# Equal SBUF offsets for all pools, and token sums made amid the first steps of the second pair

## The chip, the cores and the metric

The kernel runs on one core of one Trainium2 chip. The metric is the device time of an execution in microseconds (us); the times of several runs are given by their median. Instructions run on five engines with a queue each: TensorE (PE, with its weight loads shown apart as PEld), VectorE (DVE), ScalarE (ACT), GpSimd (POOL) and SyncE (SP), which issues the DMAs here. L211 means line 211 of the kernel.

## What is computed

One decoder layer over x of 1024 tokens by 1024 features, all in float32: a SwiGLU feed-forward with half weight, a token mixer (four heads of a gated delta rule and four of gated linear attention), a second SwiGLU, and a normalisation after each.

```python
def _swiglu(x, w_gate, w_up, w_down):
    return (jax.nn.silu(x @ w_gate) * (x @ w_up)) @ w_down
...
        x = _layer_norm(ALPHA * x + 0.5 * _swiglu(x, ffn1_w_gate[i], ffn1_w_up[i], ffn1_w_down[i]),
                        ln1_g[i], ln1_b[i])
        mix = _token_mixer(x, w_in[i], conv_w[i], a_log[i], dt_bias[i], gdn_norm_w[i],
                           w_gk[i], b_gk[i], gla_norm_w[i], w_out[i])
        x = _layer_norm(ALPHA * x + mix, ln2_g[i], ln2_b[i])
        x = _layer_norm(ALPHA * x + 0.5 * _swiglu(x, ffn2_w_gate[i], ffn2_w_up[i], ffn2_w_down[i]),
                        ln3_g[i], ln3_b[i])
```

The feed-forward width is 2816, which is 22 blocks of 128.

## The kernel before

**Products.** Every float32 operand is split into a high part, rounded to TensorE's fp32r (L131, on ScalarE), and the rest, the low part (L132, on VectorE). A product is three matmuls: high by high, high by low, low by high. Nearly all have 128 rows, 128 stationary columns and 512 moving columns. In a matmul the stationary tile is loaded first (PEld), then the moving tile streams past it. `proj` (L189, L190, L192) holds weights `wh`, `wl` and streams x (`xh`, `xl`). `down` (L211 to L213) holds a hidden tile (`gh`, `gl`; `hh`, `hl` in the middle; for one of the last blocks `fh`, `fl` stand in the place of the weights' halves) and streams the down weights `wh`, `wl`; its result is added to `acc` by VectorE (L216).

**Stages.** Blocks 0 and 1 of the first feed-forward are made plainly (block 0 by `hidden_first`, block 1 by `hidden`); then ten blocks go in pairs (`ffn_pairs`); then ten single blocks, whose second half fills the gaps of the token mixer (the middle of the program); then the second feed-forward: single blocks for one half of the tokens, five pairs, and four last blocks.

**Pairs.** Two blocks by two halves of the tokens are a 2x2 block product of gates and one of ups, made with seven projections in place of eight (Winograd's form; `PRODUCTS` lists P1 to P7). Four of the seven stream sums of x over the tokens: P3, P5 and P6 from `token_sums(q)` for q = 0 to 3, which loads four pieces of x and makes three sums, and P7 from `last_sums`, which overwrites the x tiles `xh10` to `xh13`, `xl10` to `xl13` with the differences. Each sum is split by `sum_parts`. The weights of a pair are sums too (`weight_sums`). `TURNS` sets the order of the steps of a pair by hand: g is one projection of the gates, u one of the ups, d one down step of the pair before.

```python
TURNS = "ggddddgddddgddddgddddgguuuuuuu"
```

Weights are made up to `DEEP` = 4 steps ahead of the step that asks for them.

**Order.** Each engine runs its queue in order. The framework's scheduler makes the queues: it starts from the order in which the calls in `run` issue the instructions and lets some pass others whose operands come later by its own model; the loads of `acc` are exempt (`keep_in_program_order`). Loads into scratch tiles `wr` (seven buffers) wait until a buffer is free.

**Memory.** `wt` takes a tile from a pool. Tiles are laid one behind the other in units of 32 bytes. The pools that stay open are `cp` (with `mhalf`), `xp` (`acc`, x and P7), `wp` (weights and `wr`) and `sl` (small statistics); behind them the phases open and close theirs: `fs` (token sums), `fa` and `fb` (hidden tiles of the pairs), `hp`, `mp` and others (the middle). By the addresses of the built program, the tiles of `xp` and `wp` begin 32 past a multiple of 64, those of `fs`, `fa`, `fb` and `hp` at a multiple of 64.

Of the kernel before, what the change touches and what calls it, by code (L numbers as in the profile page):

```python
# [39 lines left out]
C_END = C_SEL + 2  # L40
# [4 lines left out]
K1, K2 = 12, 8  # L45
# [5 lines left out]
LAST = 4  # L51
# [35 lines left out]
class Layer:  # L87
# [22 lines left out]
    def bank(self, tag):  # L110
        return self.ps.tile([P, HT], F32, name=self.nm(tag), tag=tag, bufs=BANKS[tag])

    def wt(self, pool, shape, tag, bufs, dt=F32):
        return pool.tile([P] + shape, dt, name=self.nm(tag), tag=tag, bufs=bufs)

    def u(self, tag, pool=None):
        return self.wt(pool or self.mp, [HT], tag, BUFS[tag])
# [26 lines left out]

    def constants(self, cp):
        nc = self.nc
        self.cst = cp.tile([P, C_END], F32, name="cst")
        self.ident = self.cst[:, C_ID:C_ID + P]
        self.lncol = cp.tile([P, 48], F32, name="lncol")
        self.msk = cp.tile([P, MASKW], U8, name="msk")  # L150
        self.small = cp.tile([P, 52], F32, name="small")
        self.rowb = cp.tile([P, 8], F32, name="rowb")
        self.wgk = cp.tile([P, 2 * P], F32, name="wgk")

    def load_constants(self):
        nc, a = self.nc, self.a
        nc.sync.dma_start(self.cst[:], a["cst"])
        nc.sync.dma_start(self.lncol[:], a["lncol"])
        for j in range(0, MASKW, HT):
            w = min(HT, MASKW - j)  # L160
            raw = self.u("wr", self.wp)
            nc.sync.dma_start(raw[:, 0:w], a["msk"][:, j:j + w])
            nc.scalar.copy(self.msk[:, j:j + w], raw[:, 0:w])
        nc.sync.dma_start(self.small[:], a["small"])
        nc.sync.dma_start(self.rowb[:], a["row"].partition_broadcast(P))
        nc.sync.dma_start(self.wgk[:], a["wgk"])
        nc.vector.tensor_scalar(self.small[:, 0:50], self.small[:, 0:50], 0.5, None, ALU.mult)
        nc.scalar.activation(self.rowb[:, 4:8], self.rowb[:, 4:8], AF.Exp)
# [6 lines left out]
        self.nc.sync.dma_start(raw, self.a["xT"][half, k])  # L175
        self.split(h[:], l[:], raw)

    def load_acc(self, c):
        self.tc.keep_in_program_order(self.nc.sync.dma_start(self.acc[c][:], self.a["x"][c]))

    def proj(self, w, half):
        nc = self.nc
# [237 lines left out]

    def sum_parts(self, n, q, t):

        pool, tags = (self.xp, (f"xh1{q}", f"xl1{q}")) if n == "P7" else (self.fs, (f"{n}{q}h", f"{n}{q}l"))
        self.sx[n, q] = [self.wt(pool, [HT], t, 1, F32R) for t in tags]
        self.split(self.sx[n, q][0][:], self.sx[n, q][1][:], t[:])

    def load(self, src):
# [11 lines left out]
        for n, t in (("P6", s2), ("P5", s1), ("P3", s4)):  # L439
            self.sum_parts(n, q, t)  # L440

    def last_sums(self):

        for q in range(KB // 2):
            s3, a21 = [self.load(self.raw_x(i, q)) for i in range(2)]
            self.nc.vector.tensor_tensor(s3[:], s3[:], a21[:], ALU.subtract)
            self.sum_parts("P7", q, s3)

    def tokens(self, n):
        x = lambda half, j: [(self.xh[half][k], self.xl[half][k]) for k in range(4 * j, 4 * j + 4)]  # L450
# [107 lines left out]
                self.split(hl[0][:], hl[1][:], raw[:])  # L558
                yield hl

    def ffn_pairs(self, idx, fs, before=None):

        gu, wd = self.a[f"gu{idx}"], self.a[f"wd{idx}"]
        order = [n for n, b in PRODUCTS]
        turns, need = [], []

        def plan(f, before, kinds):

            hid, work, asks = {}, {}, {}
            if before:  # L570
                keys = [(n, d) for d in range(2) for n in range(2)]
                asks["d"] = [keys[:2]] + [[]] * 7 + [keys[2:]] + [[]] * 7
                work["d"] = {}, before[1], self.halves_of([wd[before[0] + n] for n in range(2)])
            if f is not None:
                for up in range(2):

                    blocks = [m[:, sl] for sl in HALVES for m in (gu[f, up], gu[f + 1, up])]
                    asks["gu"[up]] = [[n] for n in order]
                    work["gu"[up]] = {}, hid, self.weight_sums(order[4:], *blocks)
            makes = {k: self.down_turns(w[0], w[1]) if k == "d" else self.project(w[0], w[1], k == "u") for k, w in work.items()}  # L580
            for make in makes.values():
                next(make)
            for kind in kinds:
                if kind in work:
                    ops, _, weights = work[kind]
                    for n in asks[kind].pop(0):
                        need.append((ops, n, weights))
                    turns.append((makes[kind], len(need)))
            return f, hid

        for f in range(fs.start, fs.stop, 2):
            before = plan(f, before, TURNS)
        plan(None, before, "d" * 16)
        made = 0
        for make, asked in turns:
            while made < min(asked + DEEP, len(need)):
                ops, n, weights = need[made]
                ops[n] = next(weights)
                made += 1
            next(make, None)  # L600

    def chunk(self, t, c):
# [447 lines left out]
        return on, half, 4 + 2 * p, 21 + 6 * p, self.small[:, 49:50]  # L1050

    def run(self):
        self.mhalf = self.cp.tile([P, 4], F32, name="mhalf")
        self.nc.gpsimd.memset(self.mhalf[:], -0.5)
        self.halo, self.S, self.SB = {}, [None] * NH, [None] * 2
        for c in range(KB):
            self.acc[c] = self.wt(self.xp, [D], f"acc{c}", 1)
        with self.phase("fs") as self.fs, self.phase("fa") as self.fx:
            self.scr = "gs", self.fx
            hs = [self.hidden_first(self.fx, ("gh", "gl"), 4)]  # L1060
            for q in range(KB // 2):
                self.token_sums(q)
            hs.append(now(self.hidden(1, 1, (0, 1), self.fx, ("gh", "gl"), 4)))
            for c in range(KB):
                self.load_acc(c)
            self.last_sums()
            self.ffn_pairs(1, range(2, K1), (0, {f"{i + 1}{j + 1}": hs[j][i] for i in range(2) for j in range(2)}))
        with self.phase("hp") as self.hp, self.phase("kp") as kp, self.phase("sp") as self.sp, self.phase("mp") as self.mp:
            self.scr = "xf", self.hp
            self.constants(kp)  # L1070
            self.load_constants()
            for k in range(KB // 2):
                self.restore(1, k)
            self.middle()
        with self.phase("fs") as self.fs, self.phase("fb") as self.fx:
            self.scr = "gs", self.fx
            for q in range(KB // 2):
                now(self.ffn(2, range(q * K2 // 4, (q + 1) * K2 // 4), 1, True))
                self.token_sums(q)
            self.last_sums()  # L1080
            self.ffn_pairs(2, range(K2, NF - LAST))
        self.last_blocks(range(NF - LAST, NF))

    def middle(self):
# [112 lines left out]
```

## Time and profile before

| | |
|---|---|
| time, median of 3 runs | 2081.43 us (2080.74 to 2082.23) |
| the profiled execution's own time | 2077.97 us |
| its span | 2075.8 us |
| TensorE busy | 2039.1 us in 10052 instructions |
| VectorE busy | 1443.4 us in 3057 |
| ScalarE busy | 785.9 us in 1553 |
| TensorE's granted clock, mean | 0.997 of full speed |
| read from HBM | 171.74 MB, 87 GB/s with what is written |

The profile is one execution. "Busy" of TensorE counts the time in which any matmul is in flight; matmuls overlap, so how quickly they follow one another is read from the starts in the timeline and not from the durations. A share of the chain is the part of the span in which that engine was what the end waited for.

### The profile page before, as it was taken

The page shows a single profiled execution, that of the slowest core. Times are in us where ns is not written, and L with a number is a line of the kernel's source. Part 1 is how long each engine was busy: PE and PEld are TensorE (multiplying, and loading weights), DVE is VectorE, ACT ScalarE, POOL GpSimd, SP SyncE. Part 2 cuts the span into 40 slices and gives each one's busy share as a digit, 9 for nine tenths or more (in the row PEclk, how much of TensorE's full clock was granted, in tenths as well). Part 3 has the DMA queues.
Part 4 walks back from the last instruction along what each step waited for, and adds up shares of the span by engine and source line. Part 5 has one row for each costly group of instructions (what it writes and reads, how often), then busy time and mean ns, then how long its engine had stood idle before and what let it go on. Part 6 is the DMA issues. An engine that isn't in the chain of part 4 may idle for free.

```text
span 2075.8 us, 27622 instructions
## 1 busy us (share of the span) xinstructions
PE 2039.1 (98%) x10052; PEld 1651.6 (80%) x10052; DVE 1443.4 (70%) x3057; ACT 785.9 (38%) x1553; POOL 54.8 (3%) x87
## 2 busy tenths in 40 slices
PE   7999999999999999999999999999999999999998
PEld 6888888888888777788788777788788788888887
DVE  6665565555688888768899888778856656556566
ACT  5333333223354444434464444343433322333332
POOL 0000000000000000000101000000000000000000
PEclk9999999999999999999999999999999999999999
DMA  8311112332322212222242222122444311112331
GB/s 305 106 46 61 52 51 62 121 94 91 101 92 81 69 60 84 64 67 91 68 147 67 72 72 72 61 72 75 139 132 132 97 56 46 62 51 87 120 114 66
DMA packets 97481, 181.94 MB, mean 88 GB/s; under 512 B 11200, under 2 KB 11712, under 8 KB 97344
## 3 DMA queue, kind: packets, MB, share of 16 engines
q1 hardware_dynamic: 97344, 180.17, 27.3%
q8 instruction: 79, 1.29, 0.3%
q14 instruction: 58, 0.48, 0.1%
HBM read 171.74 MB, written 8.39 MB: 87 GB/s over the span
## 4 chain that ended last, share of the span: by engine, by line
PE 87%; DVE 7%; ACT 2%; issue 2%; DMA 1%; POOL 1%; SPq 0%; DVEq 0%; ACTq 0%; POOLq 0%
PE pa L189 11%; PE pa L190 11%; PE pa L192 11%; PE pd L212 9%; PE pd L211 9%; PE pd L213 9%; PE pm L528 3%; PE pm L529 3%; PE pm L530 3%; PE pa L529 3%; PE pa L528 3%; PE pa L530 3%; PE pm L1019 1%; PE pm L617 1%; DVE wl L132 1%
## 5 line engine op out<-in xcount | busy, mean ns | idle before, releaser
L131 ACT CAST wh<-wr 128x512 fp32r<-128x512 f32 (+1 forms) x593 | 366.8, 620 | 891.0 <-PE pa L190 289.1
L132 DVE TENSOR_TENSOR wl<-wr,wh 128x512 fp32r<-128x512 f32 (+1 forms) x593 | 405.1, 686 | 240.7 <-ACT wh L131 238.3
L189 PE MATMUL pa<-xh,wh 128*128 128x512 f32 x1168 | 469.5, 402 | 15.0 <-ACT wh L131 6.0
L190 PE MATMUL pa<-xl,wh 128*128 128x512 f32 x1168 | 462.1, 396 | 0.1
L192 PE MATMUL pa<-xh,wl 128*128 128x512 f32 x1152 | 456.2, 396 | 0.0
L216 DVE SCALAR_TENSOR_TENSOR acc<-pd,acc 128x512 f32<-128x512 f32 x433 | 293.5, 686 | 97.4 <-PE pd L213 93.2
L189 PEld LDWEIGHTS pa<-xh,wh 128*128 128x128 f32 x1168 | 221.2, 189 | 62.8 <-ACT wh L131 6.7
L190 PEld LDWEIGHTS pa<-xl,wh 128*128 128x128 f32 x1168 | 221.1, 189 | 43.7 <-DVE xl L132 1.8
L192 PEld LDWEIGHTS pa<-xh,wl 128*128 128x128 f32 x1152 | 217.2, 189 | 43.8 <-DVE wl L132 0.5
L211 PE MATMUL pd<-wh,gh 128*128 128x512 f32 (+1 forms) x450 | 176.9, 394 | 1.2 <-ACT gh L131 1.0
L212 PE MATMUL pd<-wl,gh 128*128 128x512 f32 (+1 forms) x450 | 178.1, 396 | 0.0
L213 PE MATMUL pd<-wh,gl 128*128 128x512 f32 (+1 forms) x450 | 176.6, 393 | 0.0
L211 PE MATMUL pd<-wh,hh 128*128 128x512 f32 x352 | 142.0, 408 | 1.7 <-ACT xf L260 1.5
L212 PE MATMUL pd<-wl,hh 128*128 128x512 f32 x352 | 141.1, 401 | 1.0 <-DVE wl L132 1.0
L213 PE MATMUL pd<-wh,hl 128*128 128x512 f32 x352 | 138.4, 399 | 0.0
L211 PEld LDWEIGHTS pd<-wh,gh 128*128 128x128 f32 x450 | 84.5, 188 | 23.4 <-ACT gh L131 2.2
L213 PEld LDWEIGHTS pd<-wh,gl 128*128 128x128 f32 x450 | 84.5, 188 | 20.8 <-DVE gl L132 0.6
L212 PEld LDWEIGHTS pd<-wl,gh 128*128 128x128 f32 x450 | 84.5, 188 | 19.6
L211 PEld LDWEIGHTS pd<-wh,hh 128*128 128x128 f32 x352 | 66.3, 189 | 20.3 <-ACT hh L131 3.7
L213 PEld LDWEIGHTS pd<-wh,hl 128*128 128x128 f32 x352 | 66.0, 188 | 15.8 <-DVE hl L132 2.1
L212 PEld LDWEIGHTS pd<-wl,hh 128*128 128x128 f32 x352 | 66.5, 189 | 14.5 <-DVE wl L132 1.9
L528 PE MATMUL pm<-xh,wh 128*128 128x512 f32 x160 | 63.3, 396 | 0.0
(452 smaller groups left out, 3060.8 us busy)
## 6 DMA issues: line engine op xcount, KB each, us to landing
wr<-gu SPq DMA_DIRECT2D x263, 256.0 KB, 2.6
wr<-wd SPq DMA_DIRECT2D x132, 256.0 KB, 2.6
wr<-win SPq DMA_DIRECT2D x116, 256.0 KB, 2.6
wr<-wout SPq DMA_DIRECT2D x32, 256.0 KB, 2.6
wr<-xT SPq DMA_DIRECT2D x28, 256.0 KB, 4.9
wr<-x2d SPq DMA_DIRECT2D x28, 256.0 KB, 2.7
acc<-xT SPq DMA_DIRECT2D x16, 256.0 KB, 5.4
acc<-x SPq DMA_DIRECT2D x8, 512.0 KB, 9.3
```

The costliest lines, as they stand in the source:

```text
L131: self.nc.scalar.copy(hi, src)
L132: self.nc.vector.tensor_tensor(lo, src, hi.bitcast(F32), ALU.subtract)
L189: nc.tensor.matmul(ps[:], hi[:, sl], xh[k][:], start=(k == 0), stop=False)
L190: nc.tensor.matmul(ps[:], hi[:, sl], xl[k][:], start=False, stop=(lo is None and k == KB - 1))
L192: nc.tensor.matmul(ps[:], lo[:, sl], xh[k][:], start=False, stop=(k == KB - 1))
L211: nc.tensor.matmul(p, hh[:, sl], wh[:, ds], start=(i == 0), stop=False)
L212: nc.tensor.matmul(p, hh[:, sl], wl[:, ds], start=False, stop=False)
L213: nc.tensor.matmul(p, hl[:, sl], wh[:, ds], start=False, stop=(i == n - 1))
L216: nc.vector.scalar_tensor_tensor(acc, p, scale / ALPHA, acc, ALU.mult, ALU.add, accum_out=None if sums is None else sums[:, d:d + 1])
L528: nc.tensor.matmul(ps[:], op[0][:, sl], xh[:], start=new, stop=False, skip_group_check=True)
L529: nc.tensor.matmul(ps[:], op[0][:, sl], xl[:], start=False, stop=False, skip_group_check=True)
L530: nc.tensor.matmul(ps[:], op[1][:, sl], xh[:], start=False, stop=q == 3, skip_group_check=True)
```

## The change

Two things are changed.

First the layout. `wt` pads every tile to 16 elements (64 bytes for float32) unless it is told another unit; `mhalf` and the constants are widened likewise. By the addresses of the built program all tiles then begin at multiples of 64, those of x and weights at multiples of 128, hidden tiles 64 past one. An exception is written out: the sums P3, P5 and P6 are taken with 8 elements (32 bytes) more and the unit 8, so that high parts begin at a multiple of 64 and the low parts that follow 32 past one.

Then the order. In the first feed-forward `token_sums`, the loads of `acc` (now two halves of 256 KB each per tile) and `last_sums` are handed to `ffn_pairs` as `beside`: turn t of the steps first runs what `beside` has for t. In turns 0 to 3 these are the sums of q = t and the first halves of two `acc` tiles, in turns 6 to 9 the second halves of two and the differences of P7. So block 1's weights are loaded directly behind x. In the second feed-forward `last_sums` goes beside turns 0 to 3, behind the first weights of the pair.

```diff
-    def wt(self, pool, shape, tag, bufs, dt=F32):
-        return pool.tile([P] + shape, dt, name=self.nm(tag), tag=tag, bufs=bufs)
+    def wt(self, pool, shape, tag, bufs, dt=F32, line=16):
+
+        n = int(np.prod(shape))
+        if n % line == 0:
+            return pool.tile([P] + shape, dt, name=self.nm(tag), tag=tag, bufs=bufs)
+        t = pool.tile([P, n + -n % line], dt, name=self.nm(tag), tag=tag, bufs=bufs)[:, 0:n]
+        return t if len(shape) == 1 else t.rearrange("p (a b) -> p a b", b=shape[1])
...
-    def load_acc(self, c):
-        self.tc.keep_in_program_order(self.nc.sync.dma_start(self.acc[c][:], self.a["x"][c]))
+    def load_acc(self, c, d):
+        ds = HALVES[d]
+        self.tc.keep_in_program_order(self.nc.sync.dma_start(self.acc[c][:, ds], self.a["x"][c][:, ds]))
...
-        pool, tags = (self.xp, (f"xh1{q}", f"xl1{q}")) if n == "P7" else (self.fs, (f"{n}{q}h", f"{n}{q}l"))
-        self.sx[n, q] = [self.wt(pool, [HT], t, 1, F32R) for t in tags]
+        if n == "P7":
+            self.sx[n, q] = [self.wt(self.xp, [HT], f"x{e}1{q}", 1, F32R) for e in "hl"]
+        else:
+            self.sx[n, q] = [self.wt(self.fs, [HT + 8], f"{n}{q}{e}", 1, F32R, 8)[:, 0:HT] for e in "hl"]
...
-        for make, asked in turns:
+        for t, (make, asked) in enumerate(turns):
             while made < min(asked + DEEP, len(need)):
                 ops, n, weights = need[made]
                 ops[n] = next(weights)
                 made += 1
+            for work in beside.get(t, ()):
+                work()
             next(make, None)
...
-        self.mhalf = self.cp.tile([P, 4], F32, name="mhalf")
+        self.mhalf = self.cp.tile([P, 32], F32, name="mhalf")
...
-            for q in range(KB // 2):
-                self.token_sums(q)
             hs.append(now(self.hidden(1, 1, (0, 1), self.fx, ("gh", "gl"), 4)))
-            for c in range(KB):
-                self.load_acc(c)
-            self.last_sums()
-            self.ffn_pairs(1, range(2, K1), (0, {f"{i + 1}{j + 1}": hs[j][i] for i in range(2) for j in range(2)}))
+            hid = {f"{i + 1}{j + 1}": hs[j][i] for i in range(2) for j in range(2)}
+            beside = {t: [lambda q=t: self.token_sums(q)] for t in range(KB // 2)}
+            for t in range(4):
+                beside[t] += [lambda c=c: self.load_acc(c, 0) for c in (2 * t, 2 * t + 1)]
+                beside[6 + t] = [lambda c=c: self.load_acc(c, 1) for c in (2 * t, 2 * t + 1)]
+                beside[6 + t].append(lambda q=t: self.last_sums(q))
+            self.ffn_pairs(1, range(2, K1), (0, hid), beside)
...
-            self.last_sums()
-            self.ffn_pairs(2, range(K2, NF - LAST))
+            self.ffn_pairs(2, range(K2, NF - LAST), beside={t: [lambda q=t: self.last_sums(q)] for t in range(KB // 2)})
```

`last_sums` takes q now and does one of its four rounds per call. Lines move by five to seven: L131 and L132 become L136 and L137, L211 to L213 become L217 to L219, L328 becomes L334, L436 to L438 become L444 to L446, L446 becomes L453, L528 to L530 become L535 to L537.

How the instructions move is shown at three places. The first is VectorE at the start: before, directly behind block 0's low parts, the token sums are made (L436 to L438, and the low parts P50l, P60l, P30l), ahead of anything of block 1.

```order
L132 TENSOR_TENSOR xl_55_192<-acc_8_81,xh_54_191 128x512
L132 TENSOR_TENSOR gl_250<-gs_221,gh_249 128x512
L436 TENSOR_TENSOR wr_310<-wr_310,wr_312 128x512
L437 TENSOR_TENSOR wr_314<-wr_310,wr_314 128x512
L132 TENSOR_TENSOR P50l_326<-wr_310,P50h_325 128x512
L438 TENSOR_TENSOR wr_316<-wr_316,wr_314 128x512
L132 TENSOR_TENSOR P60l_322<-wr_314,P60h_321 128x512
L436 TENSOR_TENSOR wr_333<-wr_333,wr_335 128x512
L132 TENSOR_TENSOR P30l_330<-wr_316,P30h_329 128x512
L437 TENSOR_TENSOR wr_337<-wr_333,wr_337 128x512
```

Now they come behind block 1's up weights, amid its gate products (L334) and the weights of the pair.

```order
L137 TENSOR_TENSOR wl_473<-wr_470,wh_472 128x512
L444 TENSOR_TENSOR wr_483<-wr_483,wr_485 128x512
L137 TENSOR_TENSOR P50l_499<-wr_483,P50h_498 128x512
L334 TENSOR_TENSOR gs_347<-gs_347,pa_388 128x512
L445 TENSOR_TENSOR wr_487<-wr_483,wr_487 128x512
L137 TENSOR_TENSOR gl_415<-gs_347,gh_414 128x512
L137 TENSOR_TENSOR P60l_495<-wr_487,P60h_494 128x512
L137 TENSOR_TENSOR wl_480<-wr_476,wh_479 128x512
L446 TENSOR_TENSOR wr_489<-wr_489,wr_487 128x512
L334 TENSOR_TENSOR gs_374<-gs_374,pa_418 128x512
L137 TENSOR_TENSOR wl_525<-wr_448,wh_524 128x512
L137 TENSOR_TENSOR P30l_503<-wr_489,P30h_502 128x512
```

All of q = 0 has moved behind some forty instructions of block 0 and 1, and the others follow in the next turns. The second place is TensorE at the end of the first P6 of the pairs; P62 and P63 are its third and fourth sum. Before, the step runs through and a down step follows.

```order
L528 MATMUL pa_619<-P62h_367,wh_615 128x512
L529 MATMUL pa_619<-P62l_368,wh_615 128x512
L530 MATMUL pa_619<-P62h_367,wl_616 128x512
L528 MATMUL pa_619<-P63h_390,wh_615 128x512
L529 MATMUL pa_619<-P63l_391,wh_615 128x512
L530 MATMUL pa_619<-P63h_390,wl_616 128x512
L211 MATMUL pd_717<-wh_602,gh_306 128x512
L212 MATMUL pd_717<-wl_603,gh_306 128x512
```

Now matmuls of the step stand between those of down steps (pd), as the scheduler has placed them.

```order
L219 MATMUL pd_703<-wh_472,gl_445 128x512
L535 MATMUL pa_508<-P62h_591,wh_479 128x512
L217 MATMUL pd_722<-wh_466,gh_306 128x512
L218 MATMUL pd_722<-wl_467,gh_306 128x512
L219 MATMUL pd_722<-wh_466,gl_307 128x512
L217 MATMUL pd_722<-wh_472,gh_444 128x512
L536 MATMUL pa_508<-P62l_592,wh_479 128x512
L537 MATMUL pa_508<-P62h_591,wl_480 128x512
```

What has moved is the rest of P6 behind down steps that it preceded. The third place is VectorE where the pairs of the second feed-forward begin. Before, the differences of P7 (L446) and the low parts of P7 (`xl`) stand ahead of the product of the last single block (L328).

```order
L446 TENSOR_TENSOR wr_15052<-wr_15052,wr_15054 128x512
L132 TENSOR_TENSOR xl_3336_15040<-wr_15034,xh_3335_15039 128x512
L132 TENSOR_TENSOR xl_3340_15049<-wr_15043,xh_3339_15048 128x512
L132 TENSOR_TENSOR xl_3344_15058<-wr_15052,xh_3343_15057 128x512
L446 TENSOR_TENSOR wr_15061<-wr_15061,wr_15063 128x512
L132 TENSOR_TENSOR wl_15075<-wr_15070,wh_15074 128x512
L132 TENSOR_TENSOR xl_3348_15067<-wr_15061,xh_3347_15066 128x512
L328 TENSOR_TENSOR gs_14879<-gs_14879,pa_14893 128x512
L132 TENSOR_TENSOR wl_15083<-wr_15072,wh_15082 128x512
```

Now weight sums (L479, L480, L490) stand ahead of that product (L334), and the first difference (L453) behind it.

```order
L137 TENSOR_TENSOR wl_15047<-wr_15042,wh_15046 128x512
L479 TENSOR_TENSOR wr_15042<-wr_15050,wr_15042 128x512
L480 TENSOR_TENSOR wr_15058<-wr_15052,wr_15042 128x512
L490 TENSOR_TENSOR wr_15050<-wr_15052,wr_15050 128x512
L334 TENSOR_TENSOR gs_14887<-gs_14887,pa_14901 128x512
L137 TENSOR_TENSOR wl_15055<-wr_15044,wh_15054 128x512
L487 TENSOR_TENSOR wr_15044<-wr_15044,wr_15058 128x512
L137 TENSOR_TENSOR gl_14928<-gs_14887,gh_14927 128x512
L453 TENSOR_TENSOR wr_15074<-wr_15074,wr_15076 128x512
```

The differences have moved behind the product and its split.

## Rows read from the trace of the kernel before

**Rows 1.** The page, parts 1 and 4: TensorE's busy share; the chain's share by engine.

```profile
PE 2039.1 (98%) x10052; PEld 1651.6 (80%) x10052; DVE 1443.4 (70%) x3057; ACT 785.9 (38%) x1553; POOL 54.8 (3%) x87
...
PE 87%; DVE 7%; ACT 2%; issue 2%; DMA 1%; POOL 1%; SPq 0%; DVEq 0%; ACTq 0%; POOLq 0%
```

**Rows 2.** Windows, from:to in us; busy us and instructions of each engine, clock, DMA.

```profile
560.00:1480.00 920.00, 905.43 (x5165) 735.30 (x5165) 750.71 (x1952) 408.32 (x911) 45.67 (x63) 1.00 0.25 80
```

**Rows 3.** Timeline, TensorE: start us, us, instruction; first and last of 171 projection matmuls.

```profile
2006.19 0.39 PE L190 MATMUL pa<-xl,wh 128*128 128x512 f32 x1
...
2044.73 0.39 PE L189 MATMUL pa<-xh,wh 128*128 128x512 f32 x1
```

**Rows 4.** Timeline, TensorE: first and last of 24 down matmuls.

```profile
127.84 0.39 PE L211 MATMUL pd<-wh,gh 128*128 128x512 f32 x1
...
133.21 0.39 PE L213 MATMUL pd<-wh,gl 128*128 128x512 f32 x1
```

**Rows 5.** Timeline, TensorE: the first of 24 matmuls over sums, the first after.

```profile
1715.61 0.40 PE L528 MATMUL pm<-P60h,wh 128*128 128x512 f32 x1
...
1721.22 0.40 PE L528 MATMUL pm<-xh,wh 128*128 128x512 f32 x1
```

**Rows 6.** Timeline, TensorE: projections that follow a down step, the first, seventh and thirteenth.

```profile
158.62 0.40 PE L528 MATMUL pa<-xh,wh 128*128 128x512 f32 x1
...
160.01 0.40 PE L528 MATMUL pa<-xh,wh 128*128 128x512 f32 x1
...
161.38 0.40 PE L528 MATMUL pa<-P30h,wh 128*128 128x512 f32 x1
```

**Rows 7.** Timeline, TensorE, the last stage: six down matmuls over fh and fl, then wh.

```profile
1993.49 0.40 PE L211 MATMUL pd<-fh,gh 128*128 128x512 f32 x1
...
1994.88 0.40 PE L211 MATMUL pd<-wh,gh 128*128 128x512 f32 x1
```

**Rows 8.** Groups by line and shape, TensorE: xcount | busy, mean ns | idle before.

```profile
L211 PE MATMUL pd<-wh,gh 128*128 128x512 f32 x446 | 175.8, 395 | 1.2 <-ACT gh L131 1.0 <-DVE acc L216 0.2
...
L211 PE MATMUL pd<-wh,hh 128*128 128x512 f32 x352 | 142.0, 408 | 1.7 <-ACT xf L260 1.5 <-DVE acc L216 0.2
...
L528 PE MATMUL pa<-P60h,wh 128*128 128x512 f32 x10 | 4.0, 395 | 0.0
```

**Rows 9.** Timeline, TensorE, start: around the gap; in brackets idle before and its releaser.

```profile
29.94 0.39 PE L192 MATMUL pa<-xh,wl 128*128 128x512 f32 x1
36.36 0.79 PE L189 MATMUL pa<-xh,wh 128*128 128x512 f32 x1 [6.03 <-ACT wh L131]
...
41.31 0.39 PE L189 MATMUL pa<-xh,wh 128*128 128x512 f32 x1
```

**Rows 10.** Timeline, the DMA queue of SP, start.

```profile
13.29 17.05 SPq L429 DMA_DIRECT2D wr<-xT  x16
32.42 2.74 SPq L139 DMA_DIRECT2D wr<-gu  x4
```

**Rows 11.** Windows in that gap and behind it; PEclk is the granted clock.

```profile
30.30:36.20 5.90, 0.03 (x1) 0.00 (x0) 5.87 (x11) 2.95 (x5) 0.00 (x0) 0.85 0.82 259
36.40:41.20 4.80, 4.80 (x11) 3.56 (x12) 4.08 (x7) 2.70 (x5) 0.00 (x0) 0.50 0.89 270
```

**Rows 12.** DMA issues: size and median us from issue to landing.

```profile
wr<-gu SPq DMA_DIRECT2D x263, 256.0 KB, 2.6
...
wr<-xT SPq DMA_DIRECT2D x28, 256.0 KB, 4.9
```

**Rows 13.** Timeline, TensorE, where the second pairs begin: first and tenth of ten starts.

```profile
1618.16 0.40 PE L211 MATMUL pd<-wh,gh 128*128 128x512 f32 x1
...
1621.56 0.40 PE L211 MATMUL pd<-wh,gh 128*128 128x512 f32 x1
```

**Rows 14.** Timeline, VectorE, the same place.

```profile
1614.36 1.89 DVE L132 TENSOR_TENSOR xl<-wr,xh 128x512 fp32r<-128x512 f32 x3
...
1618.20 0.68 DVE L328 TENSOR_TENSOR gs<-gs,pa 128x512 f32<-128x512 f32 x1
```

More of the change, by code (lines that the diff above doesn't have):

```diff
@@ L146, in constants @@
         nc = self.nc
-        self.cst = cp.tile([P, C_END], F32, name="cst")
+        self.cst = cp.tile([P, C_END + -C_END % 16], F32, name="cst")[:, 0:C_END]
         self.ident = self.cst[:, C_ID:C_ID + P]
@@ L150, in constants @@
         self.msk = cp.tile([P, MASKW], U8, name="msk")
-        self.small = cp.tile([P, 52], F32, name="small")
-        self.rowb = cp.tile([P, 8], F32, name="rowb")
+        self.small = cp.tile([P, 64], F32, name="small")
+        self.rowb = cp.tile([P, 16], F32, name="rowb")
         self.wgk = cp.tile([P, 2 * P], F32, name="wgk")
@@ L163, in load_constants @@
             nc.scalar.copy(self.msk[:, j:j + w], raw[:, 0:w])
-        nc.sync.dma_start(self.small[:], a["small"])
-        nc.sync.dma_start(self.rowb[:], a["row"].partition_broadcast(P))
+        nc.sync.dma_start(self.small[:, 0:52], a["small"])
+        nc.sync.dma_start(self.rowb[:, 0:8], a["row"].partition_broadcast(P))
         nc.sync.dma_start(self.wgk[:], a["wgk"])
@@ L440, in token_sums, with last_sums @@
             self.sum_parts(n, q, t)
-    def last_sums(self):
-        for q in range(KB // 2):
-            s3, a21 = [self.load(self.raw_x(i, q)) for i in range(2)]
-            self.nc.vector.tensor_tensor(s3[:], s3[:], a21[:], ALU.subtract)
-            self.sum_parts("P7", q, s3)
+    def last_sums(self, q):
+        s3, a21 = [self.load(self.raw_x(i, q)) for i in range(2)]
+        self.nc.vector.tensor_tensor(s3[:], s3[:], a21[:], ALU.subtract)
+        self.sum_parts("P7", q, s3)
     def tokens(self, n):
@@ L559, in halves_of, with ffn_pairs @@
                 yield hl
-    def ffn_pairs(self, idx, fs, before=None):
+    def ffn_pairs(self, idx, fs, before=None, beside={}):
         gu, wd = self.a[f"gu{idx}"], self.a[f"wd{idx}"]
@@ L1060, in run @@
             hs = [self.hidden_first(self.fx, ("gh", "gl"), 4)]
-            for q in range(KB // 2):
-                self.token_sums(q)
             hs.append(now(self.hidden(1, 1, (0, 1), self.fx, ("gh", "gl"), 4)))
-            for c in range(KB):
-                self.load_acc(c)
-            self.last_sums()
-            self.ffn_pairs(1, range(2, K1), (0, {f"{i + 1}{j + 1}": hs[j][i] for i in range(2) for j in range(2)}))
+            hid = {f"{i + 1}{j + 1}": hs[j][i] for i in range(2) for j in range(2)}
[5 more added lines that the diff above has]
+            self.ffn_pairs(1, range(2, K1), (0, hid), beside)
         with self.phase("hp") as self.hp, self.phase("kp") as kp, self.phase("sp") as self.sp, self.phase("mp") as self.mp:
```

## Prediction

> **What bounds the kernel now.** I read the page first: TensorE is busy for 98% of the span and carries 87% of the chain that ended last [rows 1]. So a step pays only if it closes a gap of TensorE or shortens what its matmuls themselves take. The windows show where that does not hold: in the middle of the layer, 560 to 1480 us, TensorE is busy for 905.43 of 920 us [rows 2]; outside it for 1133.7 of 1155.8 (2039.1 and 2075.8 less these). There are thus 22 us of gaps outside the middle, and a word such as "busy" says nothing of how fast the matmuls follow one another. That is the second view, the timeline of TensorE by starts, which I read for matmuls of one shape and differing operands. A projection takes both from the pools xp and wp: 170 starts lie between 2006.19 and 2044.73, 226.7 ns each [rows 3]. A down step streams weights from wp past a stationary tile of the phase's pool: 23 starts from 127.84 to 133.21, 233.5 ns each [rows 4]. A projection over token sums streams a tile of the phase's pool past weights of wp: 24 starts from 1715.61 to 1721.22, 233.8 ns [rows 5]. All have 512 columns, one type and no wait. What differs is where the tiles begin in SBUF. By the addresses of the built program, tiles are laid out in units of 32 bytes; mhalf takes one, so that all of xp and wp begins 32 past a multiple of 64, while the pools opened behind the small tiles of sl (fs, fa, fb, hp) begin at multiples of 64. Projections thus pair equal offsets (modulo 64), downs and sums unequal ones. The last stage separates offset from line: six downs over fh and fl, whose right-hand tiles lie in the same pool as the left-hand ones, run 1993.49 to 1994.88 [rows 7], 231.7 ns each, which looks slow; but a projection that follows a down step also begins so, six starts from 158.62 to 160.01 at 231.7, and the next six at 228.3 [rows 6]. A change of kind is felt for about ten matmuls, and six downs with equal offsets behave as six projections do at that point.
>
> **The change, part by part; first the offsets.** All pools begin at multiples of 64 afterwards; only the low parts of the sums P3, P5, P6 begin 32 past one. I hold the offset modulo 64 to be what sets the pace, so a down of 512 columns gains 6.7 ns (233.4 less 226.7). Such downs are 446 + 352 + 30 for each of three lines (of the last 30, over fh, no row stands here; they are the rest of the 828), 2484 in all [rows 8]. In the middle lie 816 by the code: 240 of the ten single blocks' second half, 192 of eight blocks of the second FFN, 384 of the output projection. That leaves 1668 where TensorE is the bound: 1668 x 6.67 ns = 11.1 us. Some 50 changes from downs to projections no longer cost their start: twelve starts took 2.76 us against 12 x 226.7 = 2.72 [rows 6], 0.04 each, 2.1 in all; I take 1.0, since the other kinds (sums, small matmuls of the middle) keep changing.
>
> The sums P3, P5, P6: ten pairs of blocks' gates and ten ups [rows 8], 36 matmuls each, 720, of which two in three stream a high part (now equal) and one a low part (still unequal). Full equality would give 720 x 7.1 ns = 5.1 us. The order in a step is high, low, high, so a run of equal ones is two long, and a change is felt for ten; the row nearest to it is the alternation of six in the last stage, which runs hardly faster than the unequal pace. I take 1.1, with 0 and 5.1 as ends.
>
> In the middle 816 downs (and the small matmuls with their k, q, v from the phase's pool) become quicker by 816 x 6.67 = 5.4, with its changes 7. But TensorE waits there for 14.6 of 920 us [rows 2], for results of DVE and ScalarE that do not get earlier; I take half, 3.5, with 0 and 7 as ends.
>
> Padding adds no instruction. **Loading acc in halves** makes 16 issues of 8. They stand on SP behind the sums' loads of their turn, so what delays them is priced with these (C, below); an addition to acc that is late holds one of three banks, and two downs cover it. Beyond that I cost them at nothing.
>
> **The start.** SP issues 16 loads of x for the sums from 13.29 to 30.34 and only then, at 32.42, the gate weights of block 1 [rows 10]. TensorE's last matmul of block 0 starts at 29.94, its next at 36.36, having waited 6.03 us for ScalarE's wh [rows 9], which waited for that load. In the gap the granted clock is 0.85, behind it, from 36.4 to 41.2, 0.50, the lower level of 1.2 GHz, with TensorE busy throughout [rows 11]: eleven starts take 4.95 us (36.36 to 41.31) in place of 11 x 226.7 = 2.49. So the gap costs 6.42 less one pace (0.23) = 6.2, and the clock 2.45: 8.6 us. Afterwards block 1's weights are issued directly behind x and both go.
>
> What is late next: the sums are now made amid the pair's first steps. Walking TensorE at 226.7 ns from 30.2: block 1 ends near 52 (96 matmuls), P1 and P2 near 57, four downs near 63, then the four steps of P6, with downs in between, need sums 0 to 3 one after the other; the low part of the fourth is due near 72.4. DVE, whose 34 instructions from 52.0 on (splits, sums, gate products) take about 0.6 us each (some 4.08 for seven in that window [rows 11]), reaches it as its 31st, near 70.9: a cover of 1.5 us. But wr has seven buffers, four held by the pair's weights, so the sums' loads go through two or three, one after the other, some six links. At 2.6 us a load, as most have it, the last lands in time or 0.3 late; at 4.9, as the loads of x had it [rows 12] amid 16 others, 6 x 2.3 = 14 us more. Small waits also stand on ScalarE, where the fourth cast is behind weight casts whose buffer a down frees (0.5), and before xh13 (0.7). New waits: I take 2.0, since the DMA is nearly idle once those 16 loads are spread (ends 0 and 14). Start: 8.6 - 2.0 = 6.6.
>
> **The second pairs.** At 1618.16 to 1621.56 ten starts take 3.40 us, nine paces, 2.1 at full pace [rows 13]. DVE is then at the P7 differences and their splits (1614.36 and before) and does the product for the next down (L328) only at 1618.20 [rows 14]. With last_sums put behind it: 1.3 us. They hold up DVE then in the turns that follow, of which TensorE has five steps to cover them.
>
> **Sum:** 11.1 + 1.0 + 1.1 + 3.5 + 6.6 + 1.3 = 24.6 us. The profiled run of 2077.97 becomes 2053.4; the median of the runs shown is 3.5 higher, 2081.43, and becomes 2056.8.
>
> **The rivals.** *B: the offset is not the cause* (the kind of operand, or the pool's bank, or another period). For it: no row has the same tiles at two offsets, and the six of fh are a short run. Against it: downs and sums have their pools swapped, moving against stationary, and share the pace. Then 16.7 of the sum go, 7.9 stay: 2081.4 - 7.9 = 2073.5.
>
> A rule speaks for B. The Trainium skill, TensorE: Matmul & The Clock Gate, "Step-by-step: what each phase is for", has TensorE read the streamed and the stationary operand through two independent ports, so that loading the next weights takes no bandwidth from the running matmul. By it no pairing of addresses matters and the sum is 7.9. The rows disagree, 226.7 against 233.5 with one shape, but they differ in line and pool as well as in offset.
>
> *C: the loads of the sums are late.* As priced, at the 4.9 us of the earlier loads, 14 us; the walk's early waits overlap with it: 12 more than taken, 2056.8 + 12 = 2069. For it: the wr slots are a chain. Against it: in the second FFN the same kind of sums is made amid other steps, and the 22 us of gaps outside the middle, 6 of which are the start's, leave little room for such a loss.
>
> *D: slower: the period is 128.* Downs now begin 96 apart modulo 128, sums 32, and both cost 6.7 to 7.1 more than at 0; afterwards downs are 64 apart, which no row has. If cost rises with distance to a maximum at 64, a down takes 240 ns: 1668 x 6.7 = 11.1 lost in place of gained, 2.7 in the middle: +13.8, less 7.9 of the order: 2081.4 + 5.9 = 2087. It decides from a down pace of 237.2 on, where 2076 x 3.8 ns eat the 7.9. Against it: fh downs, 0 apart, are no proof, but a fault by halves of a line of 64 is what equal costs at 32 and 96 fit best.
>
> **How the numbers follow.** The forecast 0.70; B 0.10; C 0.12; B and C together 0.03 (2085.5); D 0.05. The forecast's own range: all of the sums, the middle and no new waits give 24.6 + 4.0 + 3.5 + 2.0 + 1.1 = 35.2, 2046; none of sums and middle and a further 6 of waits, 14.0, 2067. B and D lie above it, C in its upper part; with 2046 to 2070 I leave B, D and B with C out, 0.18. About 0.2% (4 us) is what a measurement of this kernel can tell from no change. Faster by more than it: A, B, C, 0.92; within: most of B with C, 0.03; slower: D, 0.05.
>
> **What would show it.** Down matmuls at 227 ns in any long run and half of the sums' pace unchanged: the offsets right; still 233: B; 240: D. No idle time at 30 to 36 us and a granted clock of full speed behind it: the start right; waits for P6's parts from 62 to 90 us with the DMA as releaser: C. At 1590 to 1640, no wait for DVE's gate product. The middle is wrong if its span shrinks by 7, or not at all.

## The result, and the profile after

The changed kernel takes 2063.24 us (median of 6 runs, 2060.96 to 2065.53) against 2081.04 us (6 runs): a ratio of 0.9914, 95% interval 0.9902 to 0.9927, or 17.8 us less. Forecast were 2057 us, 2046 to 2070, so 24 less. The direction and the range held. Over a quarter of the gain did not come: the rule behind the largest term, that places equal modulo 64 are enough, did not hold, and the experiments below get some 5 us back by making them equal. Of all executions behind the medians of this document one, of the kernel with a distance of 192, took 6719.77 us where its others took 2068 to 2070, and it is left out.

The profiled execution of the changed kernel took 2064.20 us with a span of 2062.4. Its page, parts 1 and 4, answers [rows 1]:

```profile
PE 2029.2 (98%) x10052; PEld 1651.0 (80%) x10052; DVE 1442.4 (70%) x3057; ACT 786.1 (38%) x1553; POOL 54.8 (3%) x87
...
PE 87%; DVE 7%; ACT 2%; DMA 2%; issue 1%; POOL 1%; SPq 0%; DVEq 0%; ACTq 0%; POOLq 0%
```

TensorE is still the bound, with the same 10052 instructions. The timeline of TensorE answers [rows 4] and [rows 5]. The first pair is the same 24 down matmuls as in [rows 4] (their first and last start), the second the same 24 matmuls over sums as in [rows 5] (the first, and the one after the last):

```profile
122.14 0.39 PE L217 MATMUL pd<-wh,gh 128*128 128x512 f32 x1
...
127.41 0.39 PE L219 MATMUL pd<-wh,gl 128*128 128x512 f32 x1
...
1704.50 0.39 PE L535 MATMUL pm<-P60h,wh 128*128 128x512 f32 x1
...
1710.06 0.39 PE L535 MATMUL pm<-xh,wh 128*128 128x512 f32 x1
```

23 starts in 5.27 us are 229.1 ns each, where [rows 4] gave 233.5 and the forecast was 226.7. 24 in 5.56 are 231.7, where [rows 5] gave 233.8. At this place the downs gain two thirds of what was forecast.

At the start the timeline of TensorE, around the moment of [rows 9]:

```profile
29.87 0.39 PE L198 MATMUL pa<-xh,wl 128*128 128x512 f32 x1
30.09 0.39 PE L195 MATMUL pa<-xh,wh 128*128 128x512 f32 x1
30.32 0.39 PE L196 MATMUL pa<-xl,wh 128*128 128x512 f32 x1
30.55 0.39 PE L198 MATMUL pa<-xh,wl 128*128 128x512 f32 x1
30.77 0.39 PE L195 MATMUL pa<-xh,wh 128*128 128x512 f32 x1
```

Block 1 follows block 0 at full pace; the 6.03 us of waiting are gone. The windows of the same stretches as in [rows 11] (from and to in us; busy us and instructions of PE, PEld, DVE, ACT, POOL; granted clock; DMA share; GB/s) and the DMA queue of SP, which answers [rows 10]:

```profile
30.30:36.20 5.90, 5.90 (x27) 4.88 (x26) 3.67 (x6) 1.25 (x2) 0.00 (x0) 1.00 0.00 1
36.40:41.20 4.80, 4.80 (x22) 3.95 (x22) 0.69 (x1) 1.22 (x2) 0.00 (x0) 1.00 0.00 0
```

```profile
13.33 2.31 SPq L144 DMA_DIRECT2D wr<-gu  x4
...
40.32 9.61 SPq L437 DMA_DIRECT2D wr<-xT  x4
```

Block 1's weights are now issued at 13.33 in place of 32.42, and the first loads for sums at 40.32. The clock is granted in full in both windows (0.85 and 0.50 before), so the slow stretch went with the gap. What is new stands later, in the timeline of TensorE and then of VectorE:

```profile
67.31 0.51 PE L535 MATMUL pa<-P62h,wh 128*128 128x512 f32 x1 [0.90 <-ACT P62h L136]
...
84.12 0.50 PE L535 MATMUL pa<-xh,wh 128*128 128x512 f32 x1 [1.29 <-ACT xh L136]
```

```profile
82.72 0.69 DVE L453 TENSOR_TENSOR wr<-wr,wr 128x512 f32<-128x512 f32 x1 [0.89 <-DMA wr<-xT]
```

TensorE waits for the third part of P6 and, at 84.12, for a part of P7, whose difference on VectorE had waited for a load. The DMA issues of these loads (first from 40 to 72 us, the sums', then from 72 to 84, P7's; KB, median us from issue to landing) and the windows of the same two stretches show which of them are slow:

```profile
wr<-xT SPq DMA_DIRECT2D x16, 256.0 KB, 2.8
...
wr<-xT SPq DMA_DIRECT2D x8, 256.0 KB, 5.6
```

```profile
40.00:72.00 32.00, 31.10 (x137) 25.22 (x136) 22.92 (x37) 11.79 (x20) 0.00 (x0) 1.00 0.62 196
72.00:84.00 12.00, 10.70 (x45) 7.92 (x44) 10.06 (x17) 5.20 (x10) 0.00 (x0) 1.00 0.92 306
```

The sums' loads land soon. Those of P7, issued together with the second halves of `acc`, take twice as long, with the DMA busy for 0.92 of the time, and the longer of the two waits hangs on one of them. Counted by TensorE's instructions, the first 192 (blocks 0 and 1) take 8.2 us less than before, the next 208 take 2.4 us more.

The middle, counted from the 2400th to the 7600th instruction of TensorE (of before and of after; windows):

```profile
570.15:1502.93 932.78, 916.28 (x5202) 743.36 (x5201) 760.66 (x1963) 408.98 (x912) 44.15 (x61) 1.00 0.25 81
```

```profile
560.74:1494.06 933.32, 915.27 (x5202) 744.72 (x5201) 760.19 (x1963) 409.11 (x912) 44.15 (x61) 1.00 0.26 81
```

It has the same length. TensorE is busy for 1.0 us less and idle for 1.5 more.

Where the second pairs begin, the timeline of VectorE answers [rows 14]: the product for the next down step now stands ahead of the first P7 difference. The 100 matmuls around it took some 24.4 us before and 23.3 now. Before, one of them had waited 1.03 us for the split of that product (TensorE of before, first lines); now none waits (VectorE of after, second lines).

```profile
1619.59 0.50 PE L211 MATMUL pd<-wh,gh 128*128 128x512 f32 x1 [1.03 <-ACT gh L131]
```

```profile
1607.91 0.68 DVE L334 TENSOR_TENSOR gs<-gs,pa 128x512 f32<-128x512 f32 x1
...
1610.44 0.68 DVE L453 TENSOR_TENSOR wr<-wr,wr 128x512 f32<-128x512 f32 x1
```

### The profile page after: what moved, and what is told of

The parts are those of the page before. It is cut to its first block, busy times and chain, and to the rows that moved or that the text cites. A ratio compares the mean times of both kernels' runs of the same rounds, so it can differ in the third digit from the quotient of the medians.

```text
span 2062.4 us, 27631 instructions
## 1 busy us (share of the span) xinstructions
PE 2029.2 (98%) x10052; PEld 1651.0 (80%) x10052; DVE 1442.4 (70%) x3057; ACT 786.1 (38%) x1553; POOL 54.8 (3%) x87
## 3 DMA queue, kind: packets, MB, share of 16 engines
q8 instruction: 79, 1.29, 0.3%
## 4 chain that ended last, share of the span: by engine, by line
PE 87%; DVE 7%; ACT 2%; DMA 2%; issue 1%; POOL 1%; SPq 0%; DVEq 0%; ACTq 0%; POOLq 0%
PE pa L195 11%; PE pa L196 11%; PE pa L198 11%; PE pd L218 9%; PE pd L217 9%; PE pd L219 9%; PE pm L535 3%; PE pm L536 3%; PE pm L537 3%; PE pa L535 3%; PE pa L536 3%; PE pa L537 3%; PE pm L1030 1%; PE pm L628 1%; DVE acc L222 1%
## 5 line engine op out<-in xcount | busy, mean ns | idle before, releaser
L136 ACT CAST wh<-wr 128x512 fp32r<-128x512 f32 (+1 forms) x593 | 367.1, 620 | 861.4 <-PE pa L196 298.3
L137 DVE TENSOR_TENSOR wl<-wr,wh 128x512 fp32r<-128x512 f32 (+1 forms) x593 | 404.5, 685 | 245.1 <-ACT wh L136 240.8
L195 PE MATMUL pa<-xh,wh 128*128 128x512 f32 x1168 | 467.9, 401 | 9.5 <-ACT xh L136 5.1
L217 PE MATMUL pd<-wh,gh 128*128 128x512 f32 (+1 forms) x450 | 176.0, 392 | 0.0
L219 PE MATMUL pd<-wh,gl 128*128 128x512 f32 (+1 forms) x450 | 175.4, 390 | 0.0
L217 PE MATMUL pd<-wh,hh 128*128 128x512 f32 x352 | 141.6, 407 | 1.6 <-ACT xf L266 1.5
L219 PE MATMUL pd<-wh,hl 128*128 128x512 f32 x352 | 138.5, 399 | 0.0
L217 PEld LDWEIGHTS pd<-wh,gh 128*128 128x128 f32 x450 | 84.5, 188 | 20.5 <-ACT gh L136 1.2
L219 PEld LDWEIGHTS pd<-wh,gl 128*128 128x128 f32 x450 | 84.5, 188 | 19.3 <-DVE gl L137 0.6
L217 PEld LDWEIGHTS pd<-wh,hh 128*128 128x128 f32 x352 | 66.3, 189 | 19.6 <-ACT hh L136 3.9
L219 PEld LDWEIGHTS pd<-wh,hl 128*128 128x128 f32 x352 | 66.6, 190 | 15.2 <-DVE hl L137 2.1
L535 PE MATMUL pa<-xh,wh 128*128 128x512 f32 x160 | 62.8, 392 | 1.3 <-ACT xh L136 1.3
```

What stands on the lines that cost most here:

```text
L136: self.nc.scalar.copy(hi, src)
L137: self.nc.vector.tensor_tensor(lo, src, hi.bitcast(F32), ALU.subtract)
L195: nc.tensor.matmul(ps[:], hi[:, sl], xh[k][:], start=(k == 0), stop=False)
L217: nc.tensor.matmul(p, hh[:, sl], wh[:, ds], start=(i == 0), stop=False)
L219: nc.tensor.matmul(p, hl[:, sl], wh[:, ds], start=False, stop=(i == n - 1))
L535: nc.tensor.matmul(ps[:], op[0][:, sl], xh[:], start=new, stop=False, skip_group_check=True)
```

## The experiments

My theory after the result: the distance between the places of the streamed and of the stationary tile sets the pace of a matmul, modulo more than 64. From the addresses of the built programs, streamed less stationary modulo 256: before 96 for downs, 160 for sums, 0 for projections; after 64 for downs, 0 for projections, and for the sums eight values: their high parts stand at 0, 64, 128 or 192, a quarter each, their low parts 32 past these.

### The layout alone, and the order alone

The first has the changed kernel's layout, with the sums, the loads of `acc` and `last_sums` where they were:

```diff
+            for q in range(KB // 2):
+                self.token_sums(q)
             hs.append(now(self.hidden(1, 1, (0, 1), self.fx, ("gh", "gl"), 4)))
...
-            self.ffn_pairs(1, range(2, K1), (0, hid), beside)
+            for c in range(KB):
+                self.load_acc(c)
+            self.last_sums()
+            self.ffn_pairs(1, range(2, K1), (0, {f"{i + 1}{j + 1}": hs[j][i] for i in range(2) for j in range(2)}))
```

> The layout of the changed kernel with the order of the one before. My theory: the pace of the matmuls gains by the layout alone; the trace of after has downs at 229.8 ns in place of 233.5 where TensorE is the bound (1668 of them: 6.2 us), sums 1.1 us and projections 0.7 us less, the middle nothing: 8.0 us, so about 2073, and the same paces (downs 229.8, high sums 231). Rival: the pace came with the order (which matmuls alternate); then downs stay at 233.5 and the time at 2081. The gap of 6 us at 30 us is there under both.

The second has the changed kernel's order with the old `wt`, `constants` and `sum_parts`:

```diff
-    def wt(self, pool, shape, tag, bufs, dt=F32, line=16):
+    def wt(self, pool, shape, tag, bufs, dt=F32):
...
-        self.mhalf = self.cp.tile([P, 32], F32, name="mhalf")
+        self.mhalf = self.cp.tile([P, 4], F32, name="mhalf")
```

> The order of the changed kernel with the layout of the one before. My theory: the start gains 8.2 and gives back 2.4 by new waits at 67 to 84 us, the second pairs gain 1.1: 6.9 us, about 2074, with downs at 233.5 ns. Rival: the order is worth more than the two single traces show, since the medians differ by 17.8 and the traces by 13.4: then 2070 or less here, and the layout's 8 us above stand.

Measured: the layout alone 2070.69 us, ratio 0.9952 (0.9940 to 0.9965), 9 us less where 8 were expected; the order alone 2073.28 us, ratio 0.9966 (0.9953 to 0.9978), 7 us less as expected, so its rival of 2070 or less did not come. With the layout alone the same 24 down matmuls start from 129.14 to 134.41, again 229.1 ns each, and TensorE still waits 5.81 us at 37.95:

```profile
129.14 0.39 PE L216 MATMUL pd<-wh,gh 128*128 128x512 f32 x1
...
134.41 0.39 PE L218 MATMUL pd<-wh,gl 128*128 128x512 f32 x1
```

```profile
37.95 0.79 PE L194 MATMUL pa<-xh,wh 128*128 128x512 f32 x1 [5.81 <-ACT wh L136]
```

With the order alone TensorE waits for nothing at 30 us, and the same 24 downs keep the pace of before, 233.5 ns:

```profile
121.37 0.39 PE L212 MATMUL pd<-wh,gh 128*128 128x512 f32 x1
...
126.74 0.39 PE L214 MATMUL pd<-wh,gl 128*128 128x512 f32 x1
```

The pace thus comes with the layout and the gap goes with the order; the two gains add up to the whole within their intervals (16 of 17.8 us). Rival B of the prediction, that the offsets do not set the pace, falls here.

### Distance 0 for the downs, then for everything

One tile of 64 bytes behind the small statistics moves the phases' pools, so that hidden tiles and weights are 0 or 256 apart modulo 512; the sums keep their eight distances. In the second kernel the sums lose their 32 bytes too, so that all of them stand at distance 0 modulo 256.

```diff
         self.nc.gpsimd.memset(self.mhalf[:], -0.5)
+        self.gap = self.sl.tile([P, 16], F32, name="gap")
+        self.nc.gpsimd.memset(self.gap[:], 0.0)
```

> The changed kernel with 64 bytes of padding behind the small statistics, so that hidden tiles begin at the same offset modulo 128 as the weights (after: 64 apart). Theory one: the distance modulo 128 sets the pace (0: 226.7, 64: 229.5, 32 and 96: 233.5): downs at 226.7 to 227 ns, 1668 x 2.8 = 4.7 us quicker than after, 2058.5. Theory two: only the distance modulo 64 counts, and the 229.5 of after comes from the alternation of stationary tiles: downs stay at 229.5, time that of after, 2063.

```diff
-            self.sx[n, q] = [self.wt(self.fs, [HT + 8], f"{n}{q}{e}", 1, F32R, 8)[:, 0:HT] for e in "hl"]
+            self.sx[n, q] = [self.wt(self.fs, [HT], f"{n}{q}{e}", 1, F32R) for e in "hl"]
```

> As the kernel with 64 bytes of padding, and the sums' low parts begin at the same offset as the high ones, so that every operand of a split matmul begins at a multiple of 128 (32 apart in after for the low parts). Theory one (distance modulo 128): sums too at 227 ns, 720 x 5.5 = 4.0 us less than the padded kernel, 2054.5. Theory two (modulo 64 only): the sums gain the same 4, as all are equal modulo 64: 2059. Rival to both: high and low part at one offset cost something of their own (the stagger was there for that): sums at 231 or more and no gain.

Measured: 2058.50 us (ratio 0.9895, 0.9881 to 0.9909) and 2053.86 us (0.9873, 0.9858 to 0.9888); expected were 2058.5 and 2054.5. The same 24 downs in the first, and the same 24 matmuls over sums in the second:

```profile
121.22 0.39 PE L217 MATMUL pd<-wh,gh 128*128 128x512 f32 x1
...
126.44 0.39 PE L219 MATMUL pd<-wh,gl 128*128 128x512 f32 x1
```

```profile
1698.16 0.39 PE L535 MATMUL pm<-P60h,wh 128*128 128x512 f32 x1
...
1703.60 0.39 PE L535 MATMUL pm<-xh,wh 128*128 128x512 f32 x1
```

5.22 us for 23 starts and 5.44 for 24 are 227.0 and 226.7 ns: the pace of projections [rows 3]. The rest that the prediction wanted of the downs is there as soon as the distance is 0, and the mixed distances of the sums, which their 32 bytes made, cost 4.6 us (the difference of the two medians). The kernel with all distances 0 modulo 256 beats the changed one by some 9 us.

### Is the period 128?

The distances so far, 0, 64, 96 and 160, do not tell a period of 128 from one of 256. Three kernels move the phases' pools on by other amounts (`gap` of 48, 24 and 32 elements in place of 16, from the kernel with all distances 0).

```diff
-        self.gap = self.sl.tile([P, 16], F32, name="gap")
+        self.gap = self.sl.tile([P, 48], F32, name="gap")
```

> The kernel with every operand at a multiple of 128, with the phases' pools 128 bytes further, so that moving and stationary tiles of downs and sums are 128 apart modulo 256. Theory one (the period is 128): paces stay at 227 ns and the time at 2054. Theory two (256 or 512): downs and sums above 229, time above 2059.

```diff
-        self.gap = self.sl.tile([P, 16], F32, name="gap")
+        self.gap = self.sl.tile([P, 24], F32, name="gap")
```

> The kernel with every operand at a multiple of 128, with the phases' pools 32 bytes further: x and weights stay at multiples of 128, hidden tiles and sums begin 32 past. Theory one (the distance counts, not the place of either): downs and sums at 233.5 ns as in before, 1668 x 6.3 and 720 x 6.9 ns slower than without: 2053.9 + 15.5 = 2069.4 at the middle unchanged, up to 2073 (the order alone) if the middle loses too. Theory two (tiles at 32 past a multiple of 64 as such are slow): the streaming of weights past hidden tiles, whose moving side is now well placed, at 230 or less, time below 2064.

Measured: 2069.22 us (ratio 0.9951, 0.9937 to 0.9964) with 128 bytes, 2071.30 us (0.9958, 0.9945 to 0.9971) with 32. The period of 128 that I expected fell: at 128 the downs start from 121.89 to 127.25, 233.0 ns each, nearly as slow as before the change.

```profile
121.89 0.40 PE L217 MATMUL pd<-wh,gh 128*128 128x512 f32 x1
...
127.25 0.40 PE L219 MATMUL pd<-wh,gl 128*128 128x512 f32 x1
```

With 32 the weights that are streamed begin at multiples of 128, as in the quick kernel, and only the stationary tiles and the sums have moved; downs and sums are back at 233 (the downs' lines below).

```profile
121.57 0.39 PE L217 MATMUL pd<-wh,gh 128*128 128x512 f32 x1
...
126.93 0.40 PE L219 MATMUL pd<-wh,gl 128*128 128x512 f32 x1
```

A streamed tile that begins at a multiple of 256 is thus quick or slow by where its stationary tile begins: the distance counts. That left 192.

```diff
-        self.gap = self.sl.tile([P, 16], F32, name="gap")
+        self.gap = self.sl.tile([P, 32], F32, name="gap")
```

> The kernel with every operand at a multiple of 128, with the phases' pools 64 bytes further, so that weights stand 192 from hidden tiles modulo 256, and sums 64 from weights. So far: 0 modulo 256 gives 227 ns, 64 gives 229.5 to 230, 32, 96, 128, 160 and 224 give 232.9 to 233.9. Theory one (the distance counts round a circle of 256): 192 is as 64, downs and sums at 229.5 to 230, 1668 x 2.5 + 720 x 2.9 ns slower than without: 2053.9 + 6.3 = 2060. Theory two (only equal, or the moving tile 64 ahead, is well): downs at 233, sums at 229.5: 2053.9 + 10 + 2 = 2066.

Measured: 2070.23 us (three executions), ratio 0.9947 (0.9927 to 0.9967). Downs and sums of this kernel, at the usual places:

```profile
122.54 0.40 PE L217 MATMUL pd<-wh,gh 128*128 128x512 f32 x1
...
127.91 0.39 PE L219 MATMUL pd<-wh,gl 128*128 128x512 f32 x1
```

```profile
1706.79 0.40 PE L535 MATMUL pm<-P60h,wh 128*128 128x512 f32 x1
...
1712.30 0.40 PE L535 MATMUL pm<-xh,wh 128*128 128x512 f32 x1
```

Downs (192) take 233.5 ns, sums (64) 229.6: the second theory, in which 64 ahead is nearly well and 192 is not. The time is some 4 us above what it expected; the profiled execution, 2067.97, is nearer. About half of that is in the projections, which outside the middle cost 2.4 us more than 226.7 ns each would, in this trace, and 0.4 in that of the kernel with all distances 0: the expectation had left out the changes from downs to projections. All settled starts of each trace together (mean over starts of one kind whose six predecessors have the same distance, intervals over 262 ns left out; over 300 starts each) give

```
streamed less stationary,      ns from start to start
modulo 256 bytes
  0     226.7 to 227.7   projections everywhere; downs and sums of the aligned kernels
 64     229.5 to 230.0   downs of after; sums of the 192 kernel 229.7
 32     233.3            sums, 32 bytes further
 96     233.5            downs of before
128     232.9, 233.9     downs and sums, 128 bytes further
160     233.8            sums of before
192     233.4            downs, 192 kernel
224     233.2            downs, 32 bytes further
```

By the addresses, two more things can be read here. The 64 of the changed kernel has the streamed tile at 0 and the stationary one at 192 modulo 256, that of the 192 kernel has them at 64 and 0; both give 229.7 ns, so the places themselves do not count. And in the kernel with all distances 0 most downs and all sums stand 256 apart modulo 512, projections 0, at 227.3, 226.8 and 227.0 ns: a period of 512 falls too.

### The new waits of the start, and a second trace of before

From the kernel with all distances 0, with one more scratch buffer:

```diff
-BUFS = {"w": 6, "h": 3, "xf": 3, "wr": 7, "f": 4,
+BUFS = {"w": 6, "h": 3, "xf": 3, "wr": 8, "f": 4,
```

> The kernel with every operand at a multiple of 128, with eight scratch buffers wr for loads in place of seven. Theory one: the waits that are new at the start (67, 73 and 84 us in after, 2.8 us together) come of the sums' loads going through the few free buffers one after the other; then they fall to about 1 us, and the time from 2053.9 to about 2052. Theory two: VectorE's queue is what is late there; then the waits stay and the time is the same within 1 us.

Measured: 2055.39 us, ratio 0.9878 (0.9861 to 0.9895), the same as with seven. In its trace the waits for sums are gone, but two others stand in their place, for the addition that frees a bank of down results:

```profile
65.83 0.50 PE L217 MATMUL pd<-wh,gh 128*128 128x512 f32 x1 [1.98 <-DVE acc L222]
...
76.41 0.50 PE L217 MATMUL pd<-wh,gh 128*128 128x512 f32 x1 [0.71 <-DVE acc L222]
```

Behind the first wait the granted clock is at its lower level, 1.2 GHz (window of that stretch):

```profile
66.60:70.10 3.50, 3.50 (x10) 2.68 (x9) 3.09 (x6) 1.43 (x3) 0.00 (x0) 0.51 0.94 231
```

Eight starts there take 3.37 us in place of 1.81. Against a start every 226.7 ns TensorE loses 5.1 us from 31 to 100 us here, 2.7 with seven buffers and 3.9 in after. Neither theory holds as written. The loads and sums do come earlier (the low part of the third P6 on VectorE at 64.49 us, at 69.03 with seven buffers), and the first addition to `acc` comes later in the same queue (65.09 against 62.52). In these two traces sums and additions share VectorE, and what is put ahead delays the other.

> The kernel before, once more, for a second trace. The middle, from the 2400th to the 7600th instruction of TensorE, took 932.8 us in before, 933.3 in after, 931.2 with the layout alone, 938.5 with the order alone, 932.3 and 932.1 with the two aligned kernels. Theory one: the middle waits for other engines and does not gain by the layout, and 938.5 is scatter: then 930 to 940 here. Theory two: the first trace of before was quick by chance and the layout gives the middle some 3 to 6 us: then 936 or more here.

Measured: 2080.84 us, span 2078.7, 3 us more than the first trace. The middle took 934.1 us. Over all traces it is 932.8 and 934.1 (before), 933.3 (after), 931.2 (layout alone), 932.3 and 932.1 (aligned), 933.6, 934.5 and 931.4 (other distances), and 936.5 (order alone). The expectation's 938.5 for the order alone was read from a window that ended 2 us late, at 1502.25 for 1500.25. So 936.5 hardly stands out, and no gain is seen beyond a scatter of 3 to 5 us; one of a microsecond or two could hide in it. Most of the 3 us between the two traces of before lies at the start: from the first matmul to block 1's last 58.3 us in place of 56.2 (58.4 with the layout alone, which has the same order).

## Why the prediction was right or wrong, point by point

**What bounds the kernel: right.** What shortened the span was the pace of matmuls and the gap at the start; TensorE's busy share stayed 98% and told neither.

**The downs, 11.1 us: mis-sized, the step that failed.** Some 6.2 us came (outside the middle the mean interval of some 1650 downs, those over 262 ns left out, went from 233.4 to 229.8). "I hold the offset modulo 64 to be what sets the pace" was the error. The evidence for it, the six downs over fh at [rows 7], had tiles a multiple of 512 apart, which is 0 modulo 64, 128 and 256 alike, and before offered only 0, 96 and 160. Nothing in the trace told 64 from 256, and the layout made 64 out of 96. With distance 0 the downs run at 227.0 to 227.4, close to the 226.7 that was forecast.

**The changes of kind, 1.0: near; the sums, 1.1: right in number, by luck.** Outside the middle projections cost 0.7 us less above 226.7 than before, sums 1.1 us less (5.0 to 3.9); low parts run at 234 ns and high ones at 231.3. But the term took all high parts as equal to their weights, and by the period of 256 three in four are not (they stand at 64, 128 or 192). So its reason, that equal high parts gain little amid unequal low ones, was not put to the test: with all distances 0 the sums cost 0.1 us above 226.7 ns each, not 3.9.

**The middle, 3.5: wrong, nothing came that the scatter lets see.** Downs there went from 233.4 to 230.6 ns and the length stayed, with 1.0 us less of busy time and 1.5 more of idle time. Half was a guess between 0 and 7. TensorE is 98% busy there, and still quicker matmuls did not shorten it; that they only wait longer for VectorE and ScalarE is likely from the idle time, and not shown by a run.

**The start, 6.6: near.** The gap and the clock behind it gave 8.2 where 8.6 were taken (10.4 against the second trace of before), the new waits cost 2.4 where 2.0 were. The trace had shown TensorE waiting for weights behind 16 loads, and the wait went when the loads were moved. Rival C, the loads 12 us late, did not come: the sums' loads, priced at 4.9 us there, landed in 2.8. The reason given for 2.0, a DMA that is nearly idle, was wrong, though: its share is 0.62 from 40 to 72 us and 0.92 while P7's loads are in flight, these take 5.6 us, and the longest new wait, 1.29 us at 84.12, is for one of them.

**The second pairs, 1.3: right,** 1.1, most of it the wait of 1.03 us that is gone.

**Rivals.** B fell by the layout alone. D was wrong in its price, since 64 apart is better than 96 and not worse; it was right that the period exceeds 64, though the period is not 128 either: at that distance downs run at 233.0 ns. The kernels with distances of 128 and 192 show what the same padding would have come to with another offset: 2069 to 2070 us, most of the layout's gain gone. The rule that spoke for B (the Trainium skill, TensorE: Matmul & The Clock Gate, "Step-by-step: what each phase is for": two independent read ports, so that a weight load takes nothing from the running matmul) is not borne out by these traces in the sense in which the prediction used it, that no pairing of addresses matters: the kernel with all distances 0 and the one with 192 run the same downs with the same weight loads, at 227 and at 233 ns. Whether it is the weight load that holds up the stream, no run here shows.

**The sum.** Traced: 6.2 + 0.7 + 1.1 + 0 + 5.8 + 1.1 = 14.9, and the two spans differ by 13.4 (16.3 with the second trace of before). The medians differ by 17.8; the first trace of before was a quick one (2077.97; the second took 2080.84). So the predicted 24.6 lost 4.9 in the downs, 3.5 in the middle and 1.3 in the other terms; the scatter of the one trace gave some 3 back.

## What to carry to other kernels

Where matmuls bound a kernel, compare the interval between starts over operands from different pools before counting instructions: here 3% of the interval of every down and sum lay in where tiles begin. An offset is a distance with a period, and a trace with two or three distances does not tell the period: make the streamed and the stationary tile of every matmul begin at the same address modulo 256, and measure one distance more before a smaller modulus is trusted. Of a stage that also waits for other engines, count nothing for quicker matmuls until a trace shows that its length moves.

## What the runs showed of the hardware

A matmul of 128 by 128 by 512 in fp32r, with its weights loaded anew each time, follows the one before in 226.7 to 227.7 ns where streamed and stationary tile begin at the same place modulo 256 bytes, in 229.5 to 230 where the streamed one lies 64 past it, and in 232.9 to 233.9 at every other distance tried (32, 96, 128, 160, 192 and 224). The granted clock was 0.995 to 0.999 of full speed over these traces. The asymmetry of 64 and 192 rests on downs at both distances and on sums at 64; sums at 192 in a long run were not tried. What in the chip makes it stays open.
